# Up and down projections as seven block products: a gated decoder step on one core

## The chip, the cores and the metric

The kernel runs on one core of one Trainium2 chip. The metric is the device time of one execution in microseconds. The kernel before has a median of 1527.77 us over three runs (1527.58 to 1528.58).

## The reference

One inference step of a one-layer decoder for 1024 prompt tokens and 64 sample tokens (8 sequences of 8), with a model width of 1024 and a feed-forward width of 4096, all in float32. The layer projects the normed input, runs a pooling branch and an attention branch, mixes them through gates, and ends with the part that this document is about:

```python
mixed = jax.nn.sigmoid(g_a) * branch_a + jax.nn.sigmoid(g_b) * branch_b
h = x + jnp.einsum('btd,de->bte', mixed, w_o)
z = jnp.einsum('btd,df->btf', rms_norm(h, ln2), w_up)
return h + jnp.einsum('btf,fd->btd', jnp.square(jax.nn.relu(z)), w_down)
```

The outputs are the new activations, the last pooling rows and the updated key and value windows.

## The kernel before, in words

All 1088 tokens stand side by side along the free dimension, features along the 128 partitions. A float32 product is formed from three TensorE passes: each operand is split into a high part that TensorE takes exactly (`F32R`) and the rest, and `gemm` adds high x high, high x low and low x high in PSUM (`PASSES`). A split is one ACT operation for the high part and one VectorE operation for the low part (`split`, lines 106 to 110). Weights come in panels of 128 x 2048 numbers, fetched in four quarters (`fetch`, line 114) and split into one of three `places`.

The work goes through stages: input projection with pooling and attention, the gates, the out projection, and the feed-forward part. TensorE's instructions run in the order in which they are written (`manual_schedule`). The other engines' orders, SyncE's queue of transfers and GpSimd's among them, come from a planner that works before the run: of the instructions that it takes to be ready, each engine gets the one written first. On the chip each engine then runs its list strictly in that order.

The tokens are cut into chunks of 384, 384 and 320 (`CHUNKS`). The out projection goes over four panels of `w_o`; for each panel, chunk and half panel (`m`) it runs 24 matmuls into `ph`, adds `x` (read with a stride of four tokens, line 1310), and squares the result for the norm. `norm_sums` (sums over features by TensorE, then a power on GpSimd, line 1281), `norm_spread` (a diagonal on VectorE and a matmul with ones, `bc`) and `split_h` come in between, chunk by chunk, through the list `todo`. The scale of the norm is not put on the activations `act`; it is multiplied in after the up product (`rbh`, line 1348).

The feed-forward part goes over 16 groups of 256 features (`NG`). A group has an up piece (`pz`: per chunk and half panel 24 matmuls over eight blocks of the model width) and a down piece (`py`: per chunk and output block 6 matmuls). Between them VectorE applies relu and the norm, ACT squares, and VectorE forms the low part (lines 1348 to 1351); after each `py` VectorE adds into `y`, which stays in SBUF (line 1367). The last group writes the rows out (line 1362). Copies of the untouched cache rows (44 transfers of about 1 MB) are issued by GpSimd's queue, each behind the mark of a weight split (`throttle`, line 1378).

## Time and profile before

| | |
|---|---|
| median of the runs | 1527.77 us |
| span of the profiled execution, first to last instruction | 1524.9 us |
| TensorE matmuls in it | 9801, busy 1509.6 us |
| out projection | 663 to 760 us |
| feed-forward part | 760 to 1520.2 us |
| after the last matmul | 4.7 us |
| granted TensorE clock, mean | 0.999 |

The profile is of one execution, whose own time is its span; the device time holds 2.9 us more than the span. PE stands for TensorE's matmuls, PEld for its weight loads, DVE for VectorE, POOL for GpSimd, SP for SyncE, whose queue issues most transfers. A group of instructions is given by its line, its operation and the tile that it writes, with its count, its busy time, the mean duration of one, and the idle time before it. Matmuls of a row overlap, so the mean duration of one is longer than the distance from one to the next.

### The profile page before, as it was taken

Reading aid. Unit: us, or ns where it says so; the run is one execution under the profiler, and the core shown is the slowest. Engines: PE = TensorE matmul, PEld = TensorE weight load, DVE = VectorE, ACT = ScalarE, POOL = GpSimd, SP = SyncE. Lnnn points to the kernel's source line nnn. Section 1 sums busy time; section 2 is a strip of 40 time slices with the busy share of each in tenths; the row PEclk is TensorE's granted clock in tenths of the full one; section 3 lists DMA queues with packets and bytes.
Section 4 is the critical chain, followed back from the end, with each engine's and each line's share of the span. In section 5 each row is a group of like instructions: output and inputs, shape, how many; then the busy total and the mean of one; then the engine's idle time right before and its main releaser. Section 6 shows DMA issues by size and latency. Waiting matters only on the chain.

```text
span 1524.9 us, 25381 instructions
## 1 busy us (share of the span) xinstructions
PE 1509.6 (99%) x9801; PEld 1457.6 (96%) x9801; DVE 869.1 (57%) x1878; ACT 506.0 (33%) x1597; POOL 204.8 (13%) x245
## 2 busy tenths in 40 slices
PE   9999999999999999999999999999999999999998
PEld 8988878888899999999999999999999999999998
DVE  7665575767754534344665565555565555655556
ACT  8566755787533222122422111121111211112100
POOL 1711355466100000100000000000000000000000
PEclk9999999999999999999999999999999999999999
DMA  5312887555455434574132232221322313222102
GB/s 198 107 45 79 229 214 201 152 135 107 112 159 187 170 130 155 144 253 166 54 107 75 87 107 68 94 95 67 108 69 92 103 62 110 93 73 101 35 7 118
DMA packets 111320, 178.13 MB, mean 117 GB/s; under 512 B 27160, under 2 KB 75614, under 8 KB 109983
## 3 DMA queue, kind: packets, MB, share of 16 engines
q1 hardware_dynamic: 105086, 126.17, 27.7%
q0 software_dynamic: 6112, 50.33, 9.8%
q8 instruction: 77, 1.26, 0.3%
q14 instruction: 45, 0.36, 0.1%
HBM read 155.41 MB, written 64.71 MB: 144 GB/s over the span
## 4 chain that ended last, share of the span: by engine, by line
PE 92%; DMA 3%; DVE 2%; ACT 1%; POOL 1%; issue 1%; SPq 1%; DVEq 0%; POOLq 0%; ACTq 0%
PE py L178 25%; PE pz L178 25%; PE pga L178 6%; PE pgb L178 6%; PE ph L178 6%; PE pqk L178 6%; PE pv L178 3%; PE pa L178 3%; PE a L295 3%; PE pb L178 2%; DMA pcv<-in_cache_kv_dram 1%; PE pq L178 1%; PE pk L178 1%; POOL pcv L818 1%; PE pl L474 0%
## 5 line engine op out<-in xcount | busy, mean ns | idle before, releaser
L178 PE MATMUL pz<-act,places 128*128 128x384 f32 (+1 forms) x2304 | 382.4, 326 | 0.0
L178 PE MATMUL py<-z,places 128*128 128x384 f32 (+1 forms) x2304 | 381.5, 327 | 0.0
L178 PEld LDWEIGHTS pz<-act,places 128*128 128x128 f32 x2304 | 379.5, 188 | 0.4
L178 PEld LDWEIGHTS py<-z,places 128*128 128x128 f32 x2304 | 379.5, 188 | 0.0
L1367 DVE TENSOR_TENSOR y<-y,py 128x384 f32<-128x384 f32 (+1 forms) x360 | 187.3, 530 | 107.9 <-PE py L178 107.4
L1349 ACT ACTIVATE z<-r 128x384 fp32r<-128x384 f32 (+1 forms) x96 | 48.7, 508 | 323.7 <-DVE r L1348 323.7
L1348 DVE SCALAR_TENSOR_TENSOR r<-pz,rbh 128x384 f32<-128x384 f32 (+1 forms) x96 | 51.2, 534 | 173.0 <-PE pz L178 173.0
L1378 POOL DMA_DIRECT2D out_kv_sample_dram<-in_cache_kv_dram x44 | 21.8, 495 | 933.4 <-ACT places L108 879.1
L108 ACT ACTIVATE places<-raw_u 128x512 fp32r<-128x512 f32 x64 | 38.4, 627 | 261.5 <-PE py L178 254.4
L178 PE MATMUL pga<-act,places 128*128 128x384 f32 (+1 forms) x576 | 99.9, 331 | 0.1
L178 PE MATMUL pgb<-act,places 128*128 128x384 f32 (+1 forms) x576 | 97.8, 326 | 0.0
L178 PEld LDWEIGHTS pga<-act,places 128*128 128x128 f32 x576 | 96.0, 190 | 1.0 <-issue 0.5
L178 PE MATMUL ph<-act,places 128*128 128x384 f32 (+1 forms) x576 | 95.9, 327 | 0.0
L178 PEld LDWEIGHTS pgb<-act,places 128*128 128x128 f32 x576 | 95.4, 188 | 0.0
L178 PEld LDWEIGHTS ph<-act,places 128*128 128x128 f32 x576 | 94.8, 188 | 0.3
L589 POOL TENSOR_TENSOR mr<-ms,mhalf 128x4 f32<-128x4 f32 (+2 forms) x39 | 52.6, 1351 | 106.5 <-DVE ms L588 106.2
L178 PE MATMUL pqk<-places,act 128*128 128x512 f32 x240 | 60.7, 402 | 1.0 <-ACT qk L594 1.0
L109 DVE TENSOR_TENSOR places<-raw_d,places 128x512 fp32r<-128x512 f32 x64 | 41.4, 689 | 28.2 <-ACT places L108 28.0
L1351 DVE TENSOR_TENSOR z<-q,z 128x384 fp32r<-128x384 f32 (+1 forms) x96 | 51.3, 535 | 8.1
L178 PEld LDWEIGHTS pqk<-places,act 128*128 128x128 f32 x240 | 44.6, 192 | 11.0 <-ACT qk L594 1.3
L794 POOL TENSOR_TENSOR pck<-pck,qs 128x256 f32<-128x256 f32 x64 | 47.5, 773 | 42.2 <-DMA pck<-in_cache_kv_dram 26.2
L1350 DVE TENSOR_TENSOR q<-r 128x384 f32<-128x384 f32 (+1 forms) x96 | 51.2, 535 | 2.7
(313 smaller groups left out, 1986.9 us busy)
## 6 DMA issues: line engine op xcount, KB each, us to landing
out_kv_sample_dram<-in_cache_kv_dram POOLq DMA_DIRECT2D x36, 960.0 KB, 5.7
raw_u<-in_w_up_dram SPq DMA_DIRECT2D x64, 256.0 KB
raw_d<-in_w_down_dram SPq DMA_DIRECT2D x64, 256.0 KB
raw_qkv<-in_w_in_dram SPq DMA_DIRECT2D x36, 256.0 KB
pck<-in_cache_kv_dram SPq DMA_DIRECT2D x32, 256.0 KB
pcv<-in_cache_kv_dram SPq DMA_DIRECT2D x32, 256.0 KB
out_kv_sample_dram<-in_cache_kv_dram POOLq DMA_DIRECT2D x8, 1008.0 KB, 5.6
mix_d<-mx SPq DMA_DIRECT2D x12, 384.0 KB
```

What stands on the lines that cost most here:

```text
L108: ins = s_.activation(dst_hi, src, AF.Copy)
L109: v_.tensor_tensor(dst_lo, src, dst_hi.bitcast(F32), op=ALU.subtract)
L178: last_mm[0] = t_.matmul(out, lhs(a, k), rhs(b, k), start=(j == 0), stop=(j == len(terms) - 1))
L295: last_mm[0] = t_.matmul(pts[m][:, :n], wt[:, a, kk, m * P:(m + 1) * P], act4[b][kk][:, :, part4(c)], start=(p == 0 and kk == 0), stop=(p ...
L589: g_.tensor_tensor(r[:n, :H], ms[:n, :H], mhalf[:n, :H], op=ALU.pow)
L794: behind_pe(g_.tensor_tensor(t[:, n], t[:, n], qs[:, :256], op=ALU.mult))
L1348: v_.scalar_tensor_tensor(r[:, :n], pzs[m][:, :n], 0.0, rbh[:, c0:c0 + n], op0=ALU.max, op1=ALU.mult)
L1349: s_.activation(z[:, m, 0, :n], r[:, :n], AF.Square)
L1350: v_.tensor_tensor(q[:, :n], r[:, :n], r[:, :n], op=ALU.mult)
L1351: v_.tensor_tensor(z[:, m, 1, :n], q[:, :n], z[:, m, 0, :n].bitcast(F32), op=ALU.subtract)
L1367: v_.tensor_tensor(yc, yc, py[:, :n], op=ALU.add)
L1378: ins = g_.dma_start(d, a)
```

## The change

The tokens are cut into two halves of 544 (`H`), each taken in two chunks of 272 (`Q`); every matmul of the out projection and of the feed-forward part has 272 columns. A PSUM tile `x` has two banks, one a chunk; there are four such tiles (`xtile`).

The out projection runs by token halves: all four panels of `w_o` and `x` for the first half, then again for the second. Each block of `h` is also stored to memory (`h_d`). The first half is normed (`normed`, now on the activations themselves), stored (`u_d`) and split while TensorE works on the second half.

Up product, group by group: the weight panel is four blocks (two halves of the model width by two of the 256 features), the activations are four (two halves of the width by two of the tokens). Instead of eight block products there are seven, in Strassen's form as Winograd wrote it, named p1 to p7. They need the activation versions T1 to T4, sums and differences of normed activations that `make_versions` forms once, after the second half's norm, and four sums of weight blocks a group, which GpSimd forms (`summed`). Every product is 24 matmuls (`products`). The results are combined as they leave PSUM. p1 and p2 of the first three groups (`FIRST`) run ahead of the rest.

After relu and square, four blocks of z and three differences of them are stored to memory (`z_d`, seven versions per group). The down product then goes version by version: for each of seven products all 16 groups accumulate in the four PSUM tiles, with z read back from memory, the weight block loaded and, in products 5, 6, 7 and 3, combined by GpSimd with blocks kept in SBUF (`kept`). After each product `post_down` evicts PSUM and combines; after product 6 it adds into `hs`, the copy of `h` that product 5 loads again; products 7 and 3 write the output rows, by token with a stride of four (`finish_row`).

`run` walks the steps of both parts: transfers are asked for up to nine steps ahead, splits and weight sums three, then the matmuls, then the evictions. `put_up` and `put_down` have five places each, `raw_tile` two tiles of two down steps each. The marks of these splits (`marks_f`) also pace the cache copies.

```diff
...
+    for j in range(2):
+        for d in range(4):
+            wt = by_k(panel(i["w_o"][d], f"o{j}{d}"))
+            xr = rr(hq_p, [P, 2, TOK], F32, name=f"xr{j}{d}", tag="xr", bufs=2)
...
+                po = xtile(f"ph{kk}_{j}")
+                for c in range(2):
+                    cs = slice(j * H + c * Q, j * H + (c + 1) * Q)
+                    gemm(po[:, c, :Q], KD, lambda s, k: wt[:, s, k, m * P:(m + 1) * P], lambda s, k: act[s][k][:, cs])
+                    if todo:
+                        todo.pop(0)()
+                v_.tensor_tensor(two(y[j][kk]), xs_of(po), by_token(xr[:, m, :], j), op=ALU.add)
+                dma_st(h_d[kk][:, half(j)], y[j][kk])
...
+        if j == 0:
+            todo += [lambda: norm_sums(0), lambda: norm_spread(0)]
+            todo.append(lambda: [normed(k, 0) for k in range(KD)])
+            todo += [lambda k=k: first_half(k) for k in range(KD)]
...
+    def put(t, src, shaped=False):
+        view = (lambda a: a.rearrange("p (k n) -> p k n", n=P)) if shaped else (lambda a: a)
+        ins = s_.activation(view(t[:, 0]), src, AF.Copy)
+        v_.tensor_tensor(view(t[:, 1]), src, view(t[:, 0]).bitcast(F32), op=ALU.subtract)
+        marks_f.append(ins)
+        return t
+    def put_up(src, shaped=False):
+        spot[0] += 1
+        return put(up_spots[spot[0] % 5], src, shaped)
+    def put_down(w, z):
+        spot[1] += 1
+        at = (8704, 0, 2112, 4224, 6336)[spot[1] % 5]
+        return (put(spots[:, at:at + 1024].rearrange("p (s n) -> p s n", s=2), w),
+                put(spots[:, at + 1024:at + 2112].rearrange("p (s n) -> p s n", s=2), z))
...
+        u11 = [again(k) for k in range(4)]
+        for k in range(4):
+            normed(k, 1)
+            v_.tensor_tensor(u11[k], u12[k], u11[k], op=ALU.subtract)
+            parts(1, k, u11[k])
+        for k in range(4):
+            normed(4 + k, 1)
+            split(act[0][4 + k][:, half(1)], act[1][4 + k][:, half(1)], u22[k])
+            g_.tensor_tensor(u12[k], u22[k], u12[k], op=ALU.subtract)
+            v_.tensor_tensor(u22[k], u22[k], u11[k], op=ALU.subtract)
+            parts(2, k, u22[k])
+        u21 = [again(4 + k) for k in range(4)]
+        for k in range(4):
+            parts(3, k, u12[k])
+        for k in range(4):
+            g_.tensor_tensor(u21[k], u21[k], u22[k], op=ALU.subtract)
+            parts(4, k, u21[k])
...
+    def products(x, A, Bv, first):
+        for c in range(2):
+            terms = [(a, b, k) for a, b in PASSES for k in range(4)]
+            for n, (a, b, k) in enumerate(terms):
+                t_.matmul(x[:, c, :Q], A[:, a, k * P:(k + 1) * P], Bv(b, k, c),
+                          start=(first and n == 0), stop=(n == len(terms) - 1), skip_group_check=not first)
...
+    def run(ahead=3, load_ahead=9):
+        n_load = n_prep = 0
+        got = {}
+        for n in range(len(queue)):
+            while n_load < min(len(queue), n + load_ahead):
+                if queue[n_load][0]:
+                    queue[n_load][0]()
+                n_load += 1
+            while n_prep < min(len(queue), n + ahead):
+                got[n_prep] = queue[n_prep][1]()
+                n_prep += 1
+            queue[n][2](got.pop(n))
+            queue[n][3]()
...
+        def first_post():
+            t = temp(1, f)
+            firsts[f] = [t, None, q["x"]]
+            s_.copy(two(t), xs_of(q["x"]))
+        def second_post():
+            t = temp(2, f)
+            s_.activation(two(t), xs_of(firsts[f][2]), AF.Relu)
+            s_.activation(t, t, AF.Square)
+            store_z(f, 0, t)
+            firsts[f][1] = t
...
+        def summed(n, a, b, op):
+            sums[n] = sum_tile(f"{n}_{f}")
+            g_.tensor_tensor(by_tile(sums[n]), a, b, op=op)
+            return put_up(sums[n])
...
+        def p5():
+            def post():
+                q["x5"] = q["x"]
+                q["s5"] = temp(4, f)
+                s_.copy(two(q["s5"]), xs_of(q["x"]))
+            step(lambda: summed(1, quarter(f, 1, 0), quarter(f, 1, 1), ALU.add),
+                 lambda A: products(xt(), A, B["T1"], True), post, (lambda: load_panel(f)) if early else None)
+        def p6():
+            def post():
+                t = firsts[f][0]
+                v_.tensor_tensor(two(t), two(t), xs_of(q["x"]), op=ALU.add)
+                q["u2"] = t
+            step(lambda: summed(2, by_tile(sums[1]), quarter(f, 0, 0), ALU.subtract),
+                 lambda A: products(xt(), A, B["T2"], True), post)
+        def p7():
+            def post():
+                q["x7"] = q["x"]
+                u3 = temp(3, f)
+                v_.tensor_tensor(two(u3), two(q["u2"]), xs_of(q["x"]), op=ALU.add)
+                g_.tensor_tensor(q["s5"], u3, q["s5"], op=ALU.add)
+                relu_squared(q["s5"])
+                store_z(f, 2, q["s5"])
+            step(lambda: summed(3, quarter(f, 0, 0), quarter(f, 1, 0), ALU.subtract),
+                 lambda A: products(xt(), A, B["T3"], True), post)
+        def p3():
+            def post():
+                z12 = temp(5, f)
+                v_.tensor_tensor(two(z12), two(q["u2"]), xs_of(q["x5"]), op=ALU.add)
+                relu_squared(z12)
+                t1, t2 = temp(3, f"t1_{f}"), temp(6, f)
+                z11, z22 = firsts[f][1], q["s5"]
+                g_.tensor_tensor(t1, z12, z11, op=ALU.subtract)
+                store_z(f, 3, t1)
+                v_.tensor_tensor(t2, z22, t1, op=ALU.subtract)
+                store_z(f, 4, t2)
+                g_.tensor_tensor(z12, z22, z12, op=ALU.subtract)
+                store_z(f, 5, z12)
+                q["t2"] = t2
+            step(lambda: summed(4, quarter(f, 0, 1), by_tile(sums[2]), ALU.subtract),
+                 lambda A: products(q["x5"], A, B["22"], False), post)
+        def p4():
+            def post():
+                z21 = q["u2"]
+                v_.tensor_tensor(two(z21), two(z21), xs_of(q["x7"]), op=ALU.add)
+                relu_squared(z21)
+                store_z(f, 1, z21)
+                t4 = temp(7, f)
+                g_.tensor_tensor(t4, z21, q["t2"], op=ALU.subtract)
+                store_z(f, 6, t4)
+            step(lambda: weights(1, 1), lambda A: products(q["x7"], A, B["T4"], False), post)
+        return p1, p5, p2, p6, p7, p3, p4
...
+    for f in range(FIRST):
+        groups[f][0]()
+        if f == 0:
+            then(lambda: norm_sums(1))
+        groups[f][2]()
+        if f == 0:
+            then(lambda: (norm_spread(1), make_versions()))
     for f in range(NG):
+        for n, p in enumerate(groups[f]):
+            if f >= FIRST or n not in (0, 2):
+                p()
...
+    def finish_row(kt, x, js):
+        for j in js:
+            if x is None:
+                s_.copy(by_token(rows[kt], j), two(hs[kt][:, half(j)]))
             else:
+                v_.tensor_tensor(by_token(rows[kt], j), two(hs[kt][:, half(j)]), xs_of(x), op=ALU.add)
+    def post_down(p, xs):
+        for t in range(4):
+            x = xs_of(xs[t])
+            if p == 2:
+                acs[t] = op.tile([P, 2, H], F32, name=f"ac{t}", tag=f"ac.{t}")
+                vws[t] = op.tile([P, 2, H], F32, name=f"vw{t}", tag=f"vw.{t}")
+                s_.copy(two(acs[t][:, 0]), x)
+            if p == 4:
+                s_.copy(two(acs[t][:, 1]), x)
+            if p == 1:
+                s_.copy(two(vws[t][:, 1]), x)
+                v_.tensor_tensor(two(acs[t][:, 0]), two(acs[t][:, 0]), x, op=ALU.add)
+            if p == 5:
+                s_.copy(two(vws[t][:, 0]), x)
+            if p == 6:
+                a, c, v, w = acs[t][:, 0], acs[t][:, 1], vws[t][:, 0], vws[t][:, 1]
+                v_.tensor_tensor(two(w), two(w), x, op=ALU.add)
+                g_.tensor_tensor(v, v, w, op=ALU.add)
+                g_.tensor_tensor(c, c, w, op=ALU.add)
+                for kt, j, s in ((t, 0, a), (t, 1, v), (4 + t, 0, c), (4 + t, 1, v)):
+                    (g_ if j else v_).tensor_tensor(hs[kt][:, half(j)], hs[kt][:, half(j)], s, op=ALU.add)
+                out_row(t, 4 + t, "ac")
+                out_row(t, t, "vw")
+                finish_row(t, None, (0,))
+            if p == 7:
+                finish_row(4 + t, xs[t], (0, 1))
+                dma_st(o["yT"][(4 + t) * P:(5 + t) * P], rows[4 + t])
+            if p == 3:
+                finish_row(t, xs[t], (1,))
+                dma_st(o["yT"][t * P:(t + 1) * P], rows[t])
+    ZI = {2: 1, 4: 6, 1: 0, 5: 3, 6: 4, 7: 5, 3: 2}
...
+        def load(f):
+            if f == 0 and p == 5:
+                for kt in range(KD):
+                    hs[kt] = op.tile([P, TOK], F32, name=f"hs{kt}")
+                    dma(hs[kt], h_d[kt])
+            if f % 2 == 0:
+                q[f] = raw_tile(f"d{p}_{f}")
+            w, z = parts(f)
+            if p == 4:
+                dma(kept[1, f], of(f, 1, 1))
+            elif p == 1:
+                dma(kept[2, f], of(f, 0, 0))
+            elif p != 6:
+                dma(w, of(f, *((1, 0) if p in (5, 7) else (0, 1))))
+            dma(z, z_d[f, :, ZI[p], :])
+        def prep(f):
+            w, z = parts(f)
+            if p in (4, 1):
+                w = kept[1 if p == 4 else 2, f]
+            elif p in (5, 6):
+                k1 = kept[1, f]
+                if p == 5:
+                    g_.tensor_tensor(k1, w, k1, op=ALU.add)
+                else:
+                    g_.tensor_tensor(k1, k1, kept[2, f], op=ALU.subtract)
+                w = k1
+            elif p == 7:
+                g_.tensor_tensor(w, kept[2, f], w, op=ALU.subtract)
+            elif p == 3:
+                g_.tensor_tensor(w, w, kept[1, f], op=ALU.subtract)
+            return put_down(w, z)
+        def mm(f, AZ):
+            A, Z = AZ
+            if f == 0:
+                q["x"] = [xtile(f"pd{p}_{t}") for t in range(4)]
+            for t in range(4):
+                for c in range(2):
+                    for n, (a, b) in enumerate(PASSES):
+                        t_.matmul(q["x"][t][:, c, :Q], A[:, a, t * P:(t + 1) * P], Z[:, b, c * Q:(c + 1) * Q],
+                                  start=(f == 0 and n == 0), stop=(f == NG - 1 and n == 2))
...
+    for p in (2, 4, 1, 5, 6, 7, 3):
+        down_stage(p)
+    run()
...
-    late = throttle[13:]
+    late = throttle[13:] + marks_f[:-20]
     for n, (d, a) in enumerate(shifts):
         ins = g_.dma_start(d, a)
-        tc.add_manual_dep(ins.ins, late[n].ins.name,
+        tc.add_manual_dep(ins.ins, late[n * len(late) // len(shifts)].ins.name,
...
```

272 lines of the change are left out of this document (176 added, 96 removed).

## The prediction

> **What bounds the kernel now.** I read the page first, then the span cut by stages, then the chain that ended last, and last the groups by shape for durations. The page:
>
> ```profile
> span 1524.9 us, 25381 instructions
> PE 1509.6 (99%) x9801; PEld 1457.6 (96%) x9801; DVE 869.1 (57%) x1878; ACT 506.0 (33%) x1597; POOL 204.8 (13%) x245
> PEclk9999999999999999999999999999999999999999
> GB/s 198 107 45 79 229 214 201 152 135 107 112 159 187 170 130 155 144 253 166 54 107 75 87 107 68 94 95 67 108 69 92 103 62 110 93 73 101 35 7 118
> q1 hardware_dynamic: 105086, 126.17, 27.7%
> ```
>
> TensorE (PE) is never free and runs at the full granted clock; VectorE (DVE) has 43% left and GpSimd (POOL) 87%. The stages, with columns span, PE, weight loads, DVE, ACT, POOL (busy us and count), granted clock, DMA share, GB/s:
>
> ```profile
> 663.00:760.00 97.00, 97.00 (x592) 96.69 (x592) 50.01 (x105) 30.36 (x58) 4.82 (x7) 1.00 0.45 158
> 760.00:1520.20 760.20, 759.82 (x4618) 758.82 (x4616) 434.63 (x833) 124.30 (x228) 15.47 (x30) 1.00 0.24 83
> 1520.20:1524.90 4.70, 0.00 (x0) 0.00 (x0) 0.75 (x2) 0.00 (x0) 0.00 (x0) 1.00 0.30 119
> ```
>
> The first row is the out projection, the second the feed-forward part (up and down), the third the tail. In both stages PE is busy for the whole stretch while POOL does nearly nothing (15 of 760 us), so what PE is spared shows in the time, and POOL is where new work can be put. PE's busy time is not its rate, though, because matmuls overlap; the rate is read from the chain, whose pieces are end to end:
>
> ```profile
> 189.13 2.86 PE pv L178 x24
> 468.56 4.16 PE pgb L178 x24
> 475.85 3.51 PE pgb L178 x24
> 1449.12 23.68 PE py L178 x144
> 1472.80 23.67 PE pz L178 x144
> ```
>
> The three short pieces have 256, 384 and 320 columns: 2.86/24 = 119.2 ns, 173.3 ns and 146.3 ns a matmul. From 320 to 384 a column costs 27.0/64 = 0.422 ns; down to 256 it is the same, and some 11 ns a matmul are fixed. For the 272 columns of the change I get 146.3 - 48 x 0.422 = 126.0 ns from above and 119.2 + 16 x 0.422 = 125.9 from below. I take 126.0: a step of 24 matmuls is 3.02 us.
>
> **What goes from PE.** Before, 16 groups have an up and a down piece: 32 x 23.68 = 757.8 us. After, up has 16 x 7 products x 24 matmuls and down 7 products x 16 groups x 24, together 5376 x 0.126 = 677.4 us: 80.4 less. It is not an eighth of 757.8 (94.7), because 5376 narrow matmuls pay the fixed part that 4608 wide ones paid. The out projection goes from 576 matmuls (x 0.1644 = 94.7) to 768 of 272 columns (96.8): 2.1 more. PE's own sum: 78.3 us less. Every stall below is set against it.
>
> **What comes to the other engines.** Durations:
>
> ```profile
> L109 DVE TENSOR_TENSOR places<-raw_u,places 128x512 fp32r<-128x512 f32 x64 | 42.4, 686 | 4.8 <-ACT places L108 4.4
> L1350 DVE TENSOR_TENSOR q<-r 128x384 f32<-128x384 f32 x64 | 35.6, 557 | 2.2
> L1350 DVE TENSOR_TENSOR q<-r 128x320 f32<-128x320 f32 x32 | 15.6, 489 | 0.6
> L1310 DVE TENSOR_TENSOR y<-ph,xr 128x272 f32<-128x272 f32 x16 | 10.1, 632 | 9.5 <-PE ph L178 5.8 <-DMA xr<-in_xT_dram 3.5
> L1310 DVE TENSOR_TENSOR y<-ph,xr 128x160 f32<-128x160 f32 x8 | 3.5, 432 | 10.4 <-PE ph L178 10.3
> L108 ACT ACTIVATE places<-raw_u 128x512 fp32r<-128x512 f32 x64 | 38.4, 627 | 261.5 <-PE py L178 254.4 <-DMA raw_u<-in_w_up_dram 7.0
> L1349 ACT ACTIVATE z<-r 128x384 fp32r<-128x384 f32 x64 | 33.5, 526 | 244.7 <-DVE r L1348 244.7
> 32.84 1.84 POOL L267 TENSOR_TENSOR xs<-xs,xs 128x768 f32<-128x768 f32 x1 [32.39 <-ACT xs L265]
> ```
>
> A DVE operation on 544 columns is 0.557 + 160 x 1.06 ns = 0.73 us; one with a stride of four (by token) is 0.632 + 272 x 1.79 ns = 1.12 us; ACT on 544 about 0.66. POOL alone takes 1.84 us for 768 elements, 2.4 ns each: 1.22 us for a block sum of 512 and 1.30 for 544.
>
> An up group (seven products, 168 matmuls, 21.2 us of PE) asks ACT for 7 splits and four passes of 544, 7.0 us. It asks DVE for 7 splits (4.8), four operations on SBUF alone (2.9) and four that read PSUM (2.9), and POOL for 4 x 1.22 + 4 x 1.30 = 10.1. Each fits alone. But DVE and POOL hinder each other:
>
> ```profile
> 32.84 16.69 POOL L267 TENSOR_TENSOR xs<-xs,xs 128x768 f32<-128x768 f32 x8 [32.39 <-ACT xs L265]
> 34.78 4.63 DVE L109 TENSOR_TENSOR places<-raw_a,places 128x512 fp32r<-128x512 f32 x2 [2.55 <-ACT places L108]
> ```
>
> Beside a busy POOL the DVE split takes 2.3 us, not 0.69: it waits for a whole POOL operation. So I add the two engines: 10.1 + 4.8 + 2.9 = 17.8 us if the PSUM readers run beside POOL, 20.7 if they exclude it too. PE has 21.2, so PE still sets the group, with 0.5 to 3.4 us to spare, and it costs some 0.3 us a group for splits that come late: 5 us in all, from 0 to 43 (the second rival). The Trainium skill, "SBUF — State Buffer", section "Who interferes with whom", speaks against this change: GpSimd and a DVE operation with two SBUF inputs exclude each other for whole instructions, and one with at most one SBUF input does not contend. The rows above agree with the first half; by the second the sum would be the 17.8.
>
> In the down stage a step of 3.02 us splits a weight block and a z block: DVE 0.69 + 0.73, ACT 1.29, and in products 5, 6, 7 and 3 a POOL sum of 1.22 as well. That is 2.64 us where DVE and POOL exclude each other; 87% of the step, 3 us in all (0 to 16). Of the queues, SP issues 11 transfers in an up group and two in a down step. POOL's shifts of the cache (0.5 us each, 44) wait for a split's mark with the block sums behind them; steps prepared ahead cover both, which costs nothing while at least one prepared step is left.
>
> ```profile
> 746.75 0.56 PE rth L1276 x6
> 756.72 1.17 POOL hr L1281
> 757.91 0.56 DVE dg L218
> L1281 POOL TENSOR_TENSOR hr<-hms,mhalf 64x1 f32<-64x1 f32 x1 | 0.8, 809 | 0.0
> 687.37 0.93 SPq L114 DMA_DIRECT2D raw_u<-in_w_up_dram  x2
> L1378 POOL DMA_DIRECT2D out_kv_sample_dram<-in_cache_kv_dram x44 | 21.8, 495 | 933.4 <-ACT places L108 879.1 <-ACT ce L684 32.7 <-DMA raw_o<-in_w_o_dram 21.5
> out_kv_sample_dram<-in_cache_kv_dram POOLq DMA_DIRECT2D x36, 960.0 KB, 5.7
> 1520.23 0.24 DVE y L1362
> ```
>
> SP's issue is 0.47 us, so 5.2 of 21.2 and 0.94 of 3.02. The remaining places where PE can stand still, one by one:
>
> The norm, twice: sums, power (1.17 and 0.81 for the odd column block), diagonal (0.56 x 640/384, about 0.85) and handovers make 3.2 us against a cover of one product, 3.02. I take 1.5 for both (0 to 4).
>
> The versions T1 to T4 of the activations: from the second norm on, PE has four early products and then p5, 5 x 3.02 = 15.1 us, before p6 needs T2. T2 stands behind 28 DVE operations (8 norms, 4 differences, 4 low parts of T1, 4 of the second half, 4 differences, 4 low parts of T2): 20.4 us. Four POOL differences between them exclude DVE for 5.2, and T3's four low parts (2.9) and p6's own split (0.69) stand in the same queue: 29.2. That is a stall of 14. With nothing of POOL in the way it is 20.4 - 15.1 = 5.3; with all 36 DVE and 8 POOL operations first (26.3 + 10.4 + 0.7) it is 22. I take 14, since the order in which they are written puts the versions ahead of p6's split.
>
> The end of product 6 in the down stage: 16 POOL adds of 544 (20.8 us) and DVE adds between them (16 x 0.7) make 32 us, and product 7's block sums stand behind them. Prepared steps cover at most eight (four split, four more loaded and summed), 24.2 us. I take 8; 0 if the adds are spread, 23 if only the three steps ahead are ready (32 - 9).
>
> Other product ends: all of PSUM belongs to one product, so the next waits for its evictions. After product 7 that is eight strided adds, 9.0 us from 2.0 before the end, where the last is wanted 2.3 after: 4.7. The other five have one short pass per tile, 0.5 each: 2.5 (together 2 to 10).
>
> The tail: the last row's strided adds, 4 x 1.12 from 2 us before PE's end, against 0.24 now: 2.3.
>
> Long stalls have a price of their own. At 389 us PE waited 2 us, and then this came:
>
> ```profile
> 391.09 0.37 PE L626 MATMUL sg0b<-qkTg0b,qkTg0b 64*128 64x128 f32 x1 [2.05 <-ACT pTg0b L648]
> 392.10:395.50 3.40, 3.40 (x12) 3.28 (x11) 1.69 (x9) 2.08 (x8) 0.00 (x0) 0.50 0.75 226
> 392.29 3.77 PE pga L178 x12
> ```
>
> The granted clock was 0.50 for 3.4 us, and twelve matmuls of 384 columns took 3.77 us in place of 2.08: 1.7 us lost. Three of my stalls (14, 8, 4.7) are longer than that wait: 5.1 (0 to 10).
>
> The sum: -78.3 + 1.5 + 14 + 8 + 4.7 + 2.5 + 5 + 3 + 2.3 + 5.1 = -32.2. The profiled span 1524.9 becomes 1492.7. The median of the runs, 1527.77, is 2.9 above that span, and I keep that: **1495.5 us**.
>
> **The rivals.** First, the stalls are hidden: version work starts early and the adds of product 6 are spread. With each place at its lower end (5.3 versions with the slow clock behind it 1.7, 2 at the product ends, 2.3 tail) the sum is -67: 1461. For it: DVE's 43% of free time; against it: the chain of 20.4 us behind one norm.
>
> Second, the ports decide (slower). If PSUM readers exclude POOL too, a group is 20.7 us, plus two places where DVE waits for a POOL result in the middle of a chain (p7 and p3, 2 x 1.30) and a shift's issue (0.4): 23.7 against 21.2. That is +40 in place of 5. A down step in the last four products becomes a chain of 1.22 + 0.63 + 0.69 + 0.73 = 3.27, +16 in place of 3, and the two long stalls go to 22 and 23, +23. Together 1495.5 + 35 + 13 + 23 = 1566. The gain is gone from 23.5 us a group on (32 + 5 over 16), the rest as forecast. For it: the 2.3 us split; against it: it needs nearly all overlap of the two engines to fail.
>
> Third, transfers come late. A down step loads 262 + 279 = 541 KB in 3.02 us, 179 GB/s, and the cache shifts (44 MB over 740 us) add 59: 238, where the busiest slice of before moved 253. At 214 GB/s (another busy slice) 155 are left, a step with both loads is 3.49 us, and 96 of them add 45: 1540. The out projection is as dense: w_o and x come twice, h and u go out, 2.7 to 3.3 MB in 12.1 us. The 4.5 MB of h that product 5 loads (15 us at 299 GB/s) lie behind up to eight steps loaded ahead (24 us); without these, 1555. Against it: queue q1 moved its 126 MB in 27.7% of the span, 299 GB/s while it was at work, with many small packets that the change does not add.
>
> Fourth, the narrow matmul could be bound by its weight load; the 256-column piece at 119.2 ns excludes that.
>
> **The numbers.** Forecast 0.53 (its own range 1475 to 1517), stalls hidden 0.15, ports 0.22, transfers 0.10. A measurement of this kernel tells 0.2% (3 us) from no change. Faster: the first two and a small part of the third case, 0.70; same 0.02; slower 0.28. For 8 in 10 the range goes from 1459, just under the first rival, to 1550, which takes in the transfers and the cheaper half of the ports.
>
> **What the profile after would show.** 5376 matmuls of 272 columns at 126 ns in the chain; PE without gaps in an up group of 21.2 us from f = 1 on; one gap of about 14 us before p6 of the first group, released by DVE or ACT; one of about 8 us in the first half of product 7, released by POOL's block sums; 5 us at its end; DMA near 240 GB/s in the down stage. The forecast is wrong if groups last over 23 us with PE waiting for splits (ports), if PE waits for raw tiles (transfers), or if the pitch is not 126 ns.

## The result and the profile after

The changed kernel takes 1537.28 us (median of four runs, 1534.52 to 1543.11); the kernel before took 1528.08 us in the same comparison. The ratio is 1.0066, with a 95% interval from 1.0045 to 1.0087. So it is slower by 0.7%, where 1495.5 us had been forecast.

Four lines of the page of the changed kernel, the same ones that were shown of before, and one of the transfers:

```profile
span 1532.7 us, 28345 instructions
PE 1459.3 (95%) x10765; PEld 1399.9 (91%) x10765; DVE 937.0 (61%) x1550; ACT 647.1 (42%) x1802; POOL 548.4 (36%) x461
PEclk9999999999999999999988999999999799999889
GB/s 198 107 45 92 215 222 197 146 134 112 112 161 148 81 100 97 100 299 256 207 121 143 213 193 172 192 188 177 196 249 382 309 170 204 221 211 191 163 271 120
q1 hardware_dynamic: 153758, 220.56, 45.5%
```

TensorE is busy 50 us less than before (1509.6), yet the span is 7.8 us longer: PE is idle for 73 us, where it had been idle for 15. The clock row falls below 9 in five slices, all from the end of the out projection on.

The stages (columns: span, PE, weight loads, DVE, ACT, POOL, clock, DMA share, GB/s):

```profile
665.00:771.80 106.80, 101.66 (x784) 101.07 (x783) 59.26 (x84) 34.52 (x56) 3.07 (x4) 0.97 0.74 254
771.80:826.40 54.60, 40.06 (x233) 38.05 (x232) 45.48 (x52) 24.23 (x42) 35.41 (x20) 0.78 0.42 138
826.40:1136.70 310.30, 310.30 (x2474) 310.30 (x2474) 212.37 (x230) 98.00 (x163) 192.75 (x130) 1.00 0.57 192
1136.70:1523.50 386.80, 350.24 (x2672) 345.94 (x2672) 233.34 (x245) 141.15 (x234) 136.64 (x108) 0.94 0.66 225
1523.50:1532.70 9.20, 2.35 (x19) 2.13 (x18) 4.02 (x4) 0.00 (x0) 0.00 (x0) 0.88 0.61 242
```

These are the out projection, the first nine steps of the up product, its other 103 steps, the down product, and the end. The third row is the change as it was meant: PE busy for 310.30 of 310.30 us, 3.01 us a step, clock 1.00, with POOL at work for 62% of it. Below, a step is 24 matmuls, counted from 0 in each product, and its time runs from its first matmul to that of the next step. The steady steps of the down product take 2.99 us. All 224 steps at these paces are 672.5 us; the two products took 754.0. The 81.5 us between are waits, and what a slowed clock adds to them, in a few places. PE's rows there (start, busy us, count, and in brackets the idle time before with its releaser), first in the out projection and the first up steps:

```profile
721.85 2.03 PE L1309 MATMUL rth<-ones,sqa 128*128 128x1 f32 x10 [4.56 <-DVE sqa L1353]
785.88 4.81 PE L1450 MATMUL pz<-act,apart 128*128 128x272 f32 x24 [2.46 <-ACT t L1522]
797.75 6.58 PE L1450 MATMUL pz<-act,places 128*128 128x272 f32 x30 [4.05 <-ACT t L1522]
809.04 4.22 PE L1450 MATMUL pz<-act,places 128*128 128x272 f32 x17 [3.73 <-DVE act L115]
818.17 8.33 PE L1450 MATMUL pz<-places,apart 128*128 128x272 f32 x42 [2.02 <-DVE places L115]
```

The first line is the first half's norm: TensorE stands before the sums over features until VectorE has added the last squares. The next two are a wait that the prediction did not have: an early p2 accumulates in the PSUM tile of its p1, so it waits until ScalarE has copied p1 out (`t`, line 1522). The last two are the versions T1 (`act`) and T2 (`places`). Steps 0 to 8 take 4.18, 4.05, 5.85, 4.65, 7.22, 5.61, 9.7, 9.77 and 3.51 us, 27.4 more than nine steady ones.

Then the down product, where product 2 ends and product 4 begins (SPq is SyncE's queue):

```profile
1171.57 8.77 SPq L1693 DMA_DIRECT2D kept<-in_w_down_dram  x11
1187.65 6.55 SPq L1686 DMA_DIRECT2D hs<-h_d  x8
1195.28 19.20 SPq L1696 DMA_DIRECT2D raw_d<-z_d  x8
1207.88 2.74 ACT L1381 ACTIVATE places<-raw_d 128x544 fp32r<-128x544 f32 x4 [10.22 <-DMA raw_d<-z_d]
1208.59 0.60 PE L1722 MATMUL pd<-places 128*128 128x272 f32 x1 [11.46 <-ACT places L1381]
```

Read from below: PE waited 11.46 us for a split, ScalarE waited 10.22 us for the z blocks, and their transfers had been issued behind eight reloads of `h` (4.5 MB) and bursts of panels for `kept`. The program asks for `h` in product 5, which begins at about 1303 us; the queue issued it 115 us earlier, where nine steps ahead would have been 27. These transfers go into fresh tiles and have nothing to wait for in the program, and the planner had put them ahead of z loads that had to wait for a buffer. Steps 15 to 18 take 6.77, 5.01, 14.62 and 5.41 us, 19.9 too many.

The later product ends (1 to 5, 6 to 7, 7 to 3) and the last row, with three lines of VectorE between them:

```profile
1302.60 2.92 PE L1722 MATMUL pd<-places 128*128 128x272 f32 x18 [1.83 <-DVE ac L1649]
1303.10 0.71 DVE L1658 TENSOR_TENSOR hs<-hs,ac 128x544 f32<-128x544 f32 x1
1307.99 17.21 PE L1722 MATMUL pd<-places 128*128 128x272 f32 x124 [2.47 <-DVE ac L1649]
1427.98 0.73 PE L1722 MATMUL pd<-places 128*128 128x272 f32 x2 [4.79 <-ACT places L1381]
1437.77 10.79 PE L1722 MATMUL pd<-places 128*128 128x272 f32 x72 [2.53 <-DVE places L1382]
1466.97 0.73 DVE L1382 TENSOR_TENSOR places<-raw_d,places 128x544 fp32r<-128x544 f32 x1 [2.68 <-ACT places L1381]
1467.61 2.09 DVE L1636 TENSOR_TENSOR row<-hs,pd 128x544 f32<-128x544 f32 x2
1469.85 1.70 PE L1722 MATMUL pd<-places 128*128 128x272 f32 x6 [2.75 <-DVE row L1636]
1523.65 4.02 DVE L1636 TENSOR_TENSOR row<-hs,pd 128x544 f32<-128x544 f32 x4 [10.78 <-PE pd L1722]
```

The three ends cost 6.8 us (steps 47 to 49), 13.1 (85 to 87) and 10.9 (95 to 97); three smaller places take 3.8 together.

At the first of them VectorE runs an addition into `hs` (line 1658) between the evictions that TensorE waits for. It belongs to product 6, but its operands were there already, `h` since the early reload, and the planner put it here. At the third VectorE is not busy but idle: it stands for 2.68 us before a split whose z block came late (ScalarE waited 4.35 us for it), and the first addition into the output row stands behind that split in its list. That addition starts 0.5 us after the product's last matmul, which ended at 1467.09.

### The profile page after: what moved, and what is told of

Read it like the earlier page. It is cut to its first block, busy times and chain, and to the rows that moved or that the text cites. A ratio compares the mean times of both kernels' runs of the same rounds, so it can differ in the third digit from the quotient of the medians.

```text
span 1532.7 us, 28345 instructions
## 1 busy us (share of the span) xinstructions
PE 1459.3 (95%) x10765; PEld 1399.9 (91%) x10765; DVE 937.0 (61%) x1550; ACT 647.1 (42%) x1802; POOL 548.4 (36%) x461
## 5 line engine op out<-in xcount | busy, mean ns | idle before, releaser
L1722 PE MATMUL pd<-places 128*128 128x272 f32 x2688 | 352.6, 294 | 36.6 <-ACT places L1381 19.9
L1722 PEld LDWEIGHTS pd<-places 128*128 128x128 f32 x2688 | 348.2, 195 | 40.9 <-ACT places L1381 21.7
L1382 DVE TENSOR_TENSOR places<-raw_d,places 128x544 fp32r<-128x544 f32 (+1 forms) x160 | 159.3, 1021 | 61.9 <-ACT places L1381 61.2
L1381 ACT ACTIVATE places<-raw_d 128x544 fp32r<-128x544 f32 (+1 forms) x160 | 98.9, 642 | 118.1 <-DMA raw_d<-z_d 53.1
L1450 PE MATMUL pz<-act,places 128*128 128x272 f32 x984 | 133.8, 295 | 8.4 <-DVE act L115 4.3
L1450 PEld LDWEIGHTS pz<-act,places 128*128 128x128 f32 x984 | 130.2, 194 | 9.1 <-DVE act L115 4.7
L1382 DVE TENSOR_TENSOR places<-kept,places 128x512 fp32r<-128x512 f32 x64 | 55.6, 869 | 82.4 <-ACT places L1381 82.3
L184 PE MATMUL ph<-act,places 128*128 128x272 f32 x768 | 99.3, 292 | 0.6 <-ACT places L114 0.6
L1450 PE MATMUL pz<-act,apart 128*128 128x272 f32 x552 | 74.2, 293 | 2.5 <-ACT t L1522 2.5
L1450 PEld LDWEIGHTS pz<-act,apart 128*128 128x128 f32 x552 | 72.2, 192 | 2.8 <-ACT t L1522 2.7
```

The lines of the kernel that those rows point to most:

```text
L184: last_mm[0] = t_.matmul(out, lhs(a, k), rhs(b, k), start=(j == 0), stop=(j == len(terms) - 1))
L1381: ins = s_.activation(view(t[:, 0]), src, AF.Copy)
L1382: v_.tensor_tensor(view(t[:, 1]), src, view(t[:, 0]).bitcast(F32), op=ALU.subtract)
L1450: t_.matmul(x[:, c, :Q], A[:, a, k * P:(k + 1) * P], Bv(b, k, c), start=(first and n == 0), stop=(n == len(terms) - 1), skip_group_check=n ...
L1722: t_.matmul(q["x"][t][:, c, :Q], A[:, a, t * P:(t + 1) * P], Z[:, b, c * Q:(c + 1) * Q], start=(f == 0 and n == 0), stop=(f == NG - 1 and ...
```

## The experiments

Each kernel is the changed one with the edit shown. Its time stands beside 1537.3 us; the kernel before took 1527.0 to 1528.1 us beside all of them, so they can be compared to about 1 us. The interval of the changed kernel itself is some 3 us to either side, and a difference of less than about 4 us cannot be told from none. Its profiled execution is its fastest (1534.5 us), so profiles show smaller gains than medians do. Each variant is planned anew, and steps far from its edit can move as well.

**Reloads of h one by one.** The eight reloads move into product 6, each behind the mark of a split (`behind` adds the dependency):

```diff
-            if f == 0 and p == 5:
-                for kt in range(KD):
-                    hs[kt] = op.tile([P, TOK], F32, name=f"hs{kt}")
-                    dma(hs[kt], h_d[kt])
+            if p == 6 and f % 2 == 0:
+                kt = f // 2
+                hs[kt] = op.tile([P, TOK], F32, name=f"hs{kt}")
+                behind(dma(hs[kt], h_d[kt]), marks_f[-1])
```

> The eight loads of h (4.5 MB) are asked for one by one in product 6, each behind a split's mark, in place of all at once. Burst theory: the wait at the change from product 2 to product 4 (raw_d loads behind the hs loads, steps of 6.8, 5.0, 14.6 and 5.4 us against 2.99) goes but for 2 to 4 us, so 15 to 18 us less than the changed kernel's 1537 us: 1519 to 1522. Rival, eviction theory (PSUM of one product must be emptied before the next starts): the wait stays, under 3 us less. Rival, transfer theory (the down stage is short of bandwidth): the burst only moves, and steps of 5 to 10 us appear in products 5 and 6.

Measured: 1518.95 us, ratio to before 0.9941 (0.9921 to 0.996), 18.3 less. PE's rows at the same place:

```profile
1184.83 0.39 PE L1726 MATMUL pd<-places 128*128 128x272 f32 x1 [3.25 <-ACT places L1381]
1185.59 29.58 PE L1726 MATMUL pd<-places 128*128 128x272 f32 x223 [0.37 <-DVE places L1382]
```

The wait of 11.46 us is gone, and steps 17 and 18 are back at 3.00 and 2.99. Without the burst the kernel is faster than the one before. In the profiled executions steps 15 to 18 give 14.2 us, and steps 47 to 49 another 3.0: the additions into `hs` now come 26 us after product 5 has begun, no longer between the evictions. At the start of product 7 5.5 us come back. Steps 15 and 16 are still 6.39 and 5.27 us: there the `kept` bursts stand ahead of the z loads.

**The additions after product 6 on VectorE:**

```diff
-                g_.tensor_tensor(v, v, w, op=ALU.add)
-                g_.tensor_tensor(c, c, w, op=ALU.add)
+                v_.tensor_tensor(v, v, w, op=ALU.add)
+                v_.tensor_tensor(c, c, w, op=ALU.add)
...
-                    (g_ if j else v_).tensor_tensor(hs[kt][:, half(j)], hs[kt][:, half(j)], s, op=ALU.add)
+                    v_.tensor_tensor(hs[kt][:, half(j)], hs[kt][:, half(j)], s, op=ALU.add)
```

> After product 6 the 16 GpSimd additions of 544 columns are done by VectorE. GpSimd theory (product 7's block sums stand behind 16 additions of 1.3 to 1.85 us): the stalls at steps 5 to 7 of product 7 (8, 6.8 and 7.4 us against 3) shrink from 13 us lost to under 4, and the kernel is 8 to 12 us faster than the changed one: 1525 to 1529. Port theory (the two engines exclude each other, whoever does the additions): VectorE becomes late instead and the gain is under 4 us. Transfer theory (SyncE issued nothing from 1417 to 1438 us): steps 5 to 7 stay long with ACT waiting for raw_d, gain under 3 us.

Measured: 1524.35 us, 0.9977 (0.9968 to 0.9987), 12.9 less.

```profile
1404.44 31.79 PE L1722 MATMUL pd<-places 128*128 128x272 f32 x252 [1.34 <-DVE vw L1654]
1438.06 0.51 PE L1722 MATMUL pd<-places 128*128 128x272 f32 x2 [1.82 <-ACT places L1381]
```

PE runs 252 matmuls on end where it had lost 13 us. Part comes back: steps 90 and 91 now take 4.97 and 6.12 us, behind VectorE's longer list. The time is what the GpSimd theory forecast, and a little more; the port theory as it was put (a gain under 4 us) falls. What the run does not separate is GpSimd's queue from its effect on VectorE, for both go with this edit. In the changed kernel VectorE's own additions in that stretch took 1.87 us each, and here 0.71:

```profile
L1658 DVE TENSOR_TENSOR hs<-hs,ac 128x544 f32<-128x544 f32 x4 | 7.5, 1873 | 0.0
```

```profile
1415.36 0.71 DVE L1658 TENSOR_TENSOR hs<-hs,ac 128x544 f32<-128x544 f32 x1
```

**Another order of the early products** (group 0 and 1 in turn, so that a p2 does not follow its own p1):

```diff
-    for f in range(FIRST):
-        groups[f][0]()
-        if f == 0:
+    for n, (f, m) in enumerate(((0, 0), (1, 0), (0, 2), (1, 2), (2, 0), (0, 1), (2, 2))):
+        groups[f][m]()
+        if n == 0:
...
```

> The early products run p1, p1, p2, p2, p1, p5, p2 in place of p1, p2 three times, so that another product lies between p1 and the p2 that adds onto the same PSUM tile (before the last p2 it is p5 of group 0). Copy theory (p2 waits for ACT's copy of p1, and ACT stands in its queue behind splits that wait for GpSimd and VectorE): the gaps of 2.7 and 4.3 us before the second and third p2 and the slow clock behind them go, 8 to 12 us less: 1525 to 1529. Version theory (PE gets to p6 sooner and waits there longer for T2 on VectorE): the same end, the gain is under 3 us.

Measured: 1534.42 us, 1.0051 (1.0034 to 1.0069), 2.9 less, which lies within the spread. The waits for the copies are gone and steps 0 to 4 take 7.5 us less, but 3.5 us of it come back by step 8, in one step of 22.65 us that waits for T1 (`act`), and 2 more in steps 12 to 19:

```profile
L1450 PE MATMUL pz<-act,places 128*128 128x272 f32 x984 | 134.0, 294 | 17.7 <-DVE act L115 10.0 <-ACT act L114 6.1 <-ACT t L1547 1.5
```

In the changed kernel that group waited 8.4 us, half of it for the copies:

```profile
L1450 PE MATMUL pz<-act,places 128*128 128x272 f32 x984 | 133.8, 295 | 8.4 <-DVE act L115 4.3 <-ACT t L1522 4.1
```

So the copies hid much of the wait for the versions: which wait is named last does not say what it would save.

**The first norm later** (two chunks later for the sums, three for the spread):

```diff
-            todo += [lambda: norm_sums(0), lambda: norm_spread(0)]
+            todo += [lambda: None, lambda: None, lambda: norm_sums(0), lambda: None, lambda: norm_spread(0)]
```

> In the out projection the first half's norm is asked for two chunks later (sums) and three chunks later (spread). Norm theory: the gap of 4.8 us before the sums at 717 us and 2.8 us of slow clock behind it go, 6 to 8 us less: 1529 to 1531. Load theory (w_o arrives late, 3.2 us of ACT's waits there): PE waits for the w_o panel instead, gain under 3 us.

Measured: 1527.28 us, 1.0007 (0.9988 to 1.0025), 10.0 less, more than expected. PE's sums, without a wait:

```profile
721.88 1.10 PE L1309 MATMUL rth<-ones,sqa 128*128 128x1 f32 x10
```

The wait had been 4.56 us; with it goes the slowed clock behind it (0.50 for 6.83 us from 721.55 on), and the out projection takes 99.8 us in place of 106.8. These 7.0 us are the edit's; the other 3 are within the spread.

**The version differences on VectorE:**

```diff
-            g_.tensor_tensor(u12[k], u22[k], u12[k], op=ALU.subtract)
+            v_.tensor_tensor(u12[k], u22[k], u12[k], op=ALU.subtract)
...
-            g_.tensor_tensor(u21[k], u21[k], u22[k], op=ALU.subtract)
+            v_.tensor_tensor(u21[k], u21[k], u22[k], op=ALU.subtract)
```

> The eight differences of the version stage that GpSimd forms (u12 and u21) go to VectorE, after the change as given otherwise. Theory (the stage waits for a chain, version sums to splits to ScalarE's copies, and GpSimd's 1.5 us operations are links of it): the first group shortens by 2 to 5 us, 1532 to 1535. Rival 1 (VectorE itself is the late engine of that stage, and gets eight operations more): 0 to 4 us longer, 1537 to 1541. Rival 2 (VectorE's operations are twice as long there because GpSimd works beside them): they go back to about half, and 8 us or more are gained, 1529 or less.

Measured: 1529.2 us, 1.0012 (0.9999 to 1.0026), 8.1 less, though VectorE has eight operations more. Steps 0 to 8 take 46.7 us in place of 54.5. The splits of T2 and T3 in the changed kernel, then in this one (busy us, mean ns):

```profile
L115 DVE TENSOR_TENSOR places<-y,places 128x544 fp32r<-128x544 f32 x8 | 10.1, 1288 | 0.0
```

```profile
L115 DVE TENSOR_TENSOR places<-y,places 128x544 fp32r<-128x544 f32 x8 | 5.5, 710 | 0.0
```

The same eight operations take 0.71 us each instead of 1.29 once GpSimd forms no differences beside them. That is the second rival of the expectation at one place. In the steady groups, where splits are prepared three steps ahead, the same two engines cost nothing (PE busy for 310.30 of 310.30 us).

**PSUM copied out early** after product 7, and the addition after product 1 from the copy:

```diff
-                v_.tensor_tensor(two(acs[t][:, 0]), two(acs[t][:, 0]), x, op=ALU.add)
+                v_.tensor_tensor(acs[t][:, 0], acs[t][:, 0], vws[t][:, 1], op=ALU.add)
...
-                finish_row(4 + t, xs[t], (0, 1))
+                for c in range(2):
+                    s_.copy(kept[2, 2 * t + c][:, :Q], xs[t][:, c, :Q])
+                for j in range(2):
+                    for c in range(2):
+                        v_.tensor_tensor(by_token(rows[4 + t], j)[:, c], two(hs[4 + t][:, half(j)])[:, c],
+                                         kept[2, 2 * t + c][:, :Q], op=ALU.add)
```

> After product 7 ScalarE copies the four PSUM tiles out into kept panels that are free by then, and VectorE's eight additions into the output rows read those copies; after product 1 the addition into ac reads the SBUF copy in vw instead of PSUM. Nothing else is changed. Theory (product 3, and product 5, wait until VectorE, which is behind with these additions, has read the PSUM tiles): steps 95 to 97 (5.9, 9.51 and 4.51 us) and 47 to 49 (4.98, 6.35 and 4.4 us) lose most of what they have over 3.0 us each, 8 to 14 us in all: 1523 to 1529. Rival (the steps wait for the splits of their operands, which stand behind the additions on VectorE in any case): the waits go over from the additions to the splits, 3 us or less, 1534 or more.

Measured: 1525.8 us, 0.9992 (0.9975 to 1.0008), 11.5 less. Steps 95 to 97 take 4.57, 5.01 and 2.99 us, and 47 to 49 take 2.99, 3.55 and 2.99: 13.5 us gained at the two places. Some comes back: in product 5 a few steps take 3.1 to 3.6 us, and its last and the first of product 6 take 5.32 and 4.64. Steps 84 to 86 take 27.9 us, where 85 to 87 had taken 22.1. That is not the copies' doing: the same steps take 28.4 and 25.6 us in the runs with another order and with the version differences on VectorE, whose edits lie elsewhere. The profiled execution (span 1532.8) is the longest of this kernel's ten (1520.62 to 1534.6), so its steps say where, and the median how much.

**Three together:** h reloads, additions, first norm.

> The three edits that each gained alone, together: the reloads of h one by one in product 6, the sixteen GpSimd additions after product 6 on VectorE, the first norm asked for two and three chunks later. If the three stalls are separate losses, the gains add: 1537.3 - 18.3 - 12.9 - 10.0 = 1496. In the run with the paced reloads alone the steps at the start of product 7 had become 5.5 us longer in sum (13.68, 7.15 and 6.79 against 7.94, 6.75 and 7.43 us), and the second edit takes that away too: then 1491. Rival: a stall taken out in one place comes back in the next, because the same queue or buffer only becomes late there; then the sum is not reached, and the time is 1505 or more.

Measured: 1504.29 us, 0.9848 (0.9834 to 0.9862). That is 33.0 of 41.2 us by the medians, between the theory and the rival, but the changed kernel's median, good to some 3 us, stands three times in that sum. In the profiled executions, from the first matmul of the out projection to the last of the down product, the three save 11.3, 8.3 and 8.2 us alone, 27.8 in sum, and 27.9 together: the gains add. What comes back is in these figures: steps 95 to 97 take 8.94, 8.9 and 4.27 us, 2.2 more than in the changed kernel, 90 and 91 5.12 and 6.21, and steps 15 and 16 have grown by 1.8. The waits of the down product, in the changed kernel and in this one (last columns: idle before, and its releasers):

```profile
L1722 PE MATMUL pd<-places 128*128 128x272 f32 x2688 | 352.6, 294 | 36.6 <-ACT places L1381 19.9 <-DVE row L1636 5.7 <-DVE places L1382 4.5
```

```profile
L1726 PE MATMUL pd<-places 128*128 128x272 f32 x2688 | 347.6, 292 | 20.6 <-DVE row L1636 8.1 <-ACT places L1381 6.6 <-DVE vw L1654 2.3
```

**All six edits:** these three, the version differences, the copies, and the `kept` loads paced like the reloads:

```diff
-                dma(kept[1, f], of(f, 1, 1))
+                behind(dma(kept[1, f], of(f, 1, 1)), marks_f[-1])
...
-                dma(kept[2, f], of(f, 0, 0))
+                behind(dma(kept[2, f], of(f, 0, 0)), marks_f[-1])
```

> All edits so far that go to a named wait: paced reloads of h, paced loads of the kept panels (each behind a split, as the reloads), the additions after product 6 on VectorE, the first norm later, the version differences on VectorE, and the copies after products 7 and 1. If the losses are separate: 1491 to 1496 for the first, third and fourth, less about 3 (versions), 10 (copies) and 5 (steps 15 and 16, which with the paced reloads were still 6.39 and 5.27 us): 1473 to 1478. Rival (VectorE, which gets 24 operations more, becomes late at the ends of the products, or the stalls move on): 1488 or more.

Measured: 1483.94 us (1481.54 to 1486.02), 0.9712 (0.9697 to 0.9727). It is 2.9% faster than the kernel before and 3.5% faster than the change as given, but 6 us short of the forecast sum's upper end.

```profile
PEclk9999999999999999999998999999999999999999
1121.53 143.64 PE L1731 MATMUL pd<-places 128*128 128x272 f32 x1152 [0.34 <-DVE t L1590]
1422.09 50.20 PE L1731 MATMUL pd<-places 128*128 128x272 f32 x384 [4.14 <-ACT kept L1664]
L1731 PE MATMUL pd<-places 128*128 128x272 f32 x2688 | 341.3, 289 | 12.2 <-ACT kept L1664 4.1 <-DVE places L1382 2.0 <-DVE vw L1654 1.5
```

Products 2, 4 and 1 run through, 1152 matmuls in 143.64 us, 124.7 ns each. Of the waits 12.2 us are left, a third of them in front of product 3, now for ScalarE's copies.

**The price of the versions.** Left out: the version sums, their rereads and splits; the products use plain quadrants.

```diff
...
-            v_.tensor_tensor(u11[k], u12[k], u11[k], op=ALU.subtract)
-            parts(1, k, u11[k])
...
-        for n in range(1, 5):
-            B[f"T{n}"] = version(*sums_at[n])
+        B["T1"], B["T2"], B["T3"], B["T4"] = B["11"], B["21"], B["22"], B["11"]
```

> Left out of the change as given: the versions themselves. The rereads of u, the sixteen differences and the four times four splits behind them are not formed, and the up products 5, 6, 7 and 4 use the quadrants that are there in any case (the output is not the reference's); the norm, the early products and all of the down product are kept. It prices the version stage by itself: in the change as given, steps 0 to 8 of the up product take 54.5 us where nine steps at 3.02 us are 27.2. If the versions are what they wait for (norm spread, version sums, splits: the prediction's 14 us, and what the copies of the early products add), 20 us or more go: 1510 to 1518. Rival (the early steps wait for the second half's norm and for ScalarE's copies between two products on one PSUM tile, with or without versions): 12 us or less, 1525 to 1533.

Measured: 1519.64 us, 0.9956 (0.994 to 0.9972), 17.6 less, between the two theories. Steps 0 to 8 take 34.9 us in place of 54.5: the versions cost 19.7, and 7.7 are the norm's own matmuls and two copies with the slow clock behind them, with or without versions. Other steps near the end of up, two above all, grew by 5 us, which was not followed up.

**A new order of the version stage** (on the six edits): T2 ahead of the split of the lower right quadrant, then T3, then T4 from a reread.

```diff
-            split(act[0][4 + k][:, half(1)], act[1][4 + k][:, half(1)], u22[k])
-            v_.tensor_tensor(u12[k], u22[k], u12[k], op=ALU.subtract)
-            v_.tensor_tensor(u22[k], u22[k], u11[k], op=ALU.subtract)
-            parts(2, k, u22[k])
+            v_.tensor_tensor(u11[k], u22[k], u11[k], op=ALU.subtract)
+            parts(2, k, u11[k])
+        for k in range(4):
+            v_.tensor_tensor(u12[k], u22[k], u12[k], op=ALU.subtract)
+            parts(3, k, u12[k])
+        for k in range(4):
+            split(act[0][4 + k][:, half(1)], act[1][4 + k][:, half(1)], u22[k])
...
```

> The kernel with all six edits (1483.9) and one more: the version stage forms T2 directly behind T1 (into the tiles of T1's difference), then the differences and splits of T3, then the splits of the lower right quadrant, and T4 from a reread into the freed tiles. With GpSimd out of that stage VectorE works without a gap from 778 to 800 us, at 0.63 to 0.71 us an operation, and steps 6 and 7 (8.36 and 10.79 us) wait for it. Eight operations fewer stand ahead of T2: 5 us. Theory (VectorE's order sets the start of product 6): steps 6 and 7 lose 3 to 6 us in sum, 1478 to 1481. Rival (product 7's T3 becomes the late one, or ScalarE's hi parts are as late): 2 us or less, 1482 to 1485.

Measured: 1486.76 us, 0.9737 (0.9722 to 0.9751), 2.8 more than without it (the intervals just touch) where 3 to 6 less had been expected. Steps 6 and 7 do fall, from 19.2 to 15.1 us, but ScalarE's copy of an early p1 comes later (it had cost 0.78 us of wait at this product), and steps 4 and 5 grow by 5.7:

```profile
789.96 8.45 PE L1454 MATMUL pz<-act,places 128*128 128x272 f32 x48 [4.29 <-ACT t L1526]
```

**The same with the early products in turn**, so that this copy is not waited for:

> As the kernel before in this call (all six edits and the new order of the version stage), and the early products interleaved by group (1, 1, 2, 2 of groups 0 and 1, then 1 of group 2, 5 of group 0, 2 of group 2), which alone gained 2.9 us. If the copies between two products on one PSUM tile still cost here (steps 2 and 3 of the up product take 5.78 and 3.11 us, 2.9 over two steps): 2 to 3 us less than that kernel, 1475 to 1479. Rival (the versions end when VectorE and ScalarE are done, whatever TensorE does before): the wait moves into product 5, within 1 us of that kernel.

Measured: 1483.62 us, 0.9714 (0.9698 to 0.973): 3.1 less than the run above, with intervals that overlap, and the same as the six edits without any new order (1483.94). The wait has moved into product 5, one step of 16.12 us, as the rival has it, and steps 0 to 8 take 49.3 us in place of 50.1. With every order tried, this stage of the six edits keeps 19 to 23 us over nine steady steps. That its chain is too long for the early products that there are is the likely reason; no run shows it.

**The clock by itself.**

```diff
+                for _ in range({4: 12, 7: 15, 10: 18, 13: 24}.get(f, 0)):
+                    v_.tensor_tensor(z21, z21, z21, op=ALU.max)
```

> The clock by itself: in the steady part of the up product, at the end of groups 4, 7, 10 and 13, VectorE takes the larger of a tile and itself 12, 15, 18 and 24 times (results unchanged), 8, 10, 12 and 16 us at 0.65 us each. The splits of the next three steps stand behind them, with some 6 to 9 us of cover, so TensorE is stopped four times, by about 0 to 1, 1 to 3, 3 to 5 and 7 to 9 us, each between long stretches without any wait. Theory (a stop of about 2 us or more costs half clock afterwards): windows of granted clock 0.5 and 3.4 us or more follow the longer three, each taking 1.7 us more than the stop itself, and none follows a stop below 2 us. Rival (the half clock comes from several stops close together, as they stand in the first group and at the product ends): no window after an isolated stop of 2 to 5 us, and the loss is the stop.

Measured: 1549.76 us in one run. TensorE was stopped four times, for 1.8, 1.8, 1.8 and 3.1 us, and not for four different times as meant. The first two (24 matmuls a row), and below them the windows (span, PE busy, clock, DMA share, GB/s) around the first, second, third and fourth:

```profile
918.18 3.19 PE L1450 MATMUL pz<-act,places 128*128 128x272 f32 x24
923.15 4.80 PE L1450 MATMUL pz<-t,places 128*128 128x272 f32 x24 [1.78 <-DVE t L1563]
985.02 3.19 PE L1450 MATMUL pz<-act,places 128*128 128x272 f32 x24
989.99 3.29 PE L1450 MATMUL pz<-t,apart 128*128 128x272 f32 x24 [1.79 <-DVE t L1563]
```

```profile
920.20:923.60 3.40, 1.62 (x13) 1.00 0.57 194
923.60:927.00 3.40, 3.40 (x17) 0.50 0.35 135
988.40:991.90 3.50, 1.91 (x15) 1.00 0.83 281
991.90:995.30 3.40, 3.40 (x29) 1.00 0.21 81
1053.30:1056.70 3.40, 1.60 (x13) 1.00 0.00 0
1056.70:1060.10 3.40, 3.40 (x18) 0.50 0.04 14
1121.60:1125.00 3.40, 0.56 (x4) 1.00 0.18 69
1125.00:1128.40 3.40, 3.40 (x17) 0.50 0.00 0
```

An isolated stop is enough, so the rival falls; but the theory's limit of 2 us is wrong too. Two stops of equal length differ: behind the first, 24 matmuls took 4.80 us, behind the second 3.29. What differs is where they lie on a fixed grid of 3.4 us. PE was busy for 1.62 us in the window of the first and 1.60 in that of the third; the next window ran at 0.50 and cost 1.6 us. In the window of the second it was busy for 1.91, as part of the stop fell into the window before, and the next one ran at full clock.

The line between the two is not sharp. In the traces of the changed kernel and of all its variants, cut along this grid from 600 us on, a window at full clock with at most 1.5 us of TensorE work was always followed by one at 0.50, and one with more than 2.0 us never. Between them both occur: full clock after 1.59 us (1448.90 us, the run without versions) and half after 1.96 us (797.30 us, this run). What decides there stays open; the ends of matmuls are modelled in the profile. The way back is longer: full clock returned only after a slow window with 2.89 us or more of work, so that a place where waits follow one another stays slow, in the changed kernel for up to 13.65 us.

The three half-speed windows begin 133.1 and 68.3 us apart. The Trainium skill, "TensorE: Matmul & The Clock Gate", section "Part 1: The HAM clock gate", gives a free-running window of 3413 ns; 39 and 20 of these fit, so the trace agrees. Its section "HAM oscillation — how this bites in real kernels" puts the harmful gap at over some 3.4 us; here 1.8 us was enough, and the measurement decides.

## Why the prediction was wrong

By the prediction's own steps, in the profiled execution (forecast span 1492.7, measured 1532.7):

| step | forecast, us | measured | where it was tested |
|---|---|---|---|
| 224 steps of TensorE | 677.4 | 672.5 | steady steps 3.01 and 2.99 |
| steady up groups, down steps, late splits | 5 + 3 | 0 | no gap from 826 to 1136 us |
| out projection with the first norm | 99.9 | 106.8 | first norm later |
| first up group: second norm, versions | 14.8 | 27.4 | versions left out, on VectorE, orders |
| reloads of `h`, `kept` loads (product 2 to 4) | 0 | 19.9 | reloads paced, then both |
| additions after product 6 | 8 | 13.1 | additions on VectorE |
| end of product 7 | 4.7 | 10.9 | copied out early |
| other product ends | 2.5 | 10.6 | copied out early (product 1) |
| slow clock | 5.1 | 28, in the rows above | stops put in |
| after the last matmul | 7.0 | 6.9 | |

The first row, which carried the argument, is right, and so is its companion: the pitch of 126 ns and a steady group in which GpSimd's 10 us of sums stay hidden. The ports rival was wrong about these groups. The places of the stalls were right as well: the first norm, the versions, products 6 and 7. What failed is their price, on nearly every line, one line that was priced at nothing, and the clock. Of the three gaps that the profile was to show, the one of 14 us before p6 is not there as one (the longest wait is 4.05 us, before an early p2); the other two are, but larger.

**The step that failed first is the reload of `h`.** The text put 4.5 MB at 15 us and then at 0, as they "lie behind up to eight steps loaded ahead". That assumed that the queue issues them where the program asks for them. The planner put them where product 2 ends, ahead of the z loads of steps that were due. TensorE was already waiting for splits there (3.62 us at 1188.96 us), so no step was loaded ahead when they came. The 15 us that the third rival names for this case is near the 14.2 us that steps 15 to 18 gained with paced loads, and the 18.3 us of the whole run. That rival's other half, transfers held to 214 GB/s, did not come: the page has slices of 382 and 309 in the down product. Had only this step been right, the kernel would have been faster than before, at 1519 us, and the forecast still some 23 us too low.

**The versions** were priced at 14 us, as VectorE's queue alone, with VectorE and GpSimd excluding each other for four differences; leaving them out saved 19.7. The slowing beside GpSimd was there and longer: the versions' splits took 1.3 us each. And the copy of p1 that p2 waits for, and ScalarE's order behind it, were not in the working at all.

**The ends of the products** were priced by the operations of the product that ends, done as its tiles become ready. But the evictions stand in VectorE's list with other work. After product 1 additions of product 6 stood between them, and after product 7 the first one stood behind a split that waited for its z block: it began 0.5 us after the last matmul, where the working had it 2.0 us before. For product 6 the working counts 16 additions on VectorE, where the program has 12; by its own rule the stall would have been 5 us and not 8, and 13.1 were lost.

**The clock** was charged to three stalls longer than 2 us, 5.1 us. From the first norm to its last matmul the changed kernel has eleven stretches at 0.50, 75.1 us in all, and TensorE was at work for 56.2 us of them. At full clock that work would have taken half as long, so the slow clock cost about 28 us, an estimate from these two numbers. TensorE's own account agrees: it was to be busy 78.3 us less than before and was busy 50.3 us less. Here the steps that failed are the count of the stops, three in place of eleven slow stretches, and the limit of 2 us: the run with stops put in shows a slow window behind a stop of 1.8 us.

The range, 1459 to 1550, did hold the time, but by luck: its upper end was drawn for a shortage of bandwidth and for the ports, above all in the steady groups, and neither came there. The chance of 0.28 for slower lay mostly on the ports. They showed at the versions and perhaps behind product 6; the rest of the time came from the bursts, from the order of the queues and from the clock. With six edits and the same products the kernel takes 1484 us, nearly 12 below the forecast. That shows that the saving on TensorE is real, not that the forecast's stalls were right.

## What to carry to other kernels

A saving on the engine that bounds a kernel is had only as far as every hand-over around it still keeps ahead: sum the steady state, then price each start and end separately, with the queue of every engine as it stands when that point comes, and not as it would be after a pause. A transfer "asked for later" in the program is not issued later unless something holds it back; bursts that wait for nothing go ahead of loads that are due, and a dependency on work of the right time was worth 18 us. Work that becomes ready early can also be put into an engine's list ahead of what another engine waits for. Where TensorE is the bound, count its stops and not only their length: here a window of 3.4 us with less than 1.5 us of work made the next one run at half speed, and the slow clock took about 28 us in all.
